# Seven products for the first up-projection pair of MLP groups 2 to 6, and second rounded copies in PSUM

## The chip, the cores and the metric

The kernel runs on one core of one Trainium2 chip. The metric is the device time of one execution in microseconds (us); less is better. Before the change it took 1220.0 us, the median of three runs (1218.8 to 1220.02). Five engines matter: TensorE (PE, with its weight loads as PEld) multiplies, VectorE (DVE) and ScalarE (ACT) do elementwise work, GpSimd (POOL) does elementwise work in parallel with them, and SyncE (SP) issues the transfers from HBM. Operands stand in SBUF; matmul results go to eight PSUM banks of 128 x 512 fp32 values.

## The reference

Two decoder layers on 512 tokens of width 1024: attention in layer 0, a gated short convolution in layer 1, each followed by the same MLP with 4096 hidden features, and a gated per-layer embedding. What the change touches is the MLP:

```
def sq_relu_mlp(h, w_up, w_down):
    return jnp.square(jax.nn.relu(h @ w_up)) @ w_down
for i in range(DEPTH):                              # DEPTH = 2
    ...                                             # mixer
    f = sq_relu_mlp(rmsnorm(x, g[2]), w_mlp_up[i], w_mlp_down[i])
    x = x + rmsnorm(f, g[3])
    ...                                             # gated embedding
```

Everything is fp32. The kernel reaches that precision on TensorE with rounded fp32 operands: each operand is split into a rounded part and the rest.

## The kernel before

**Three matmuls per product.** `mm3` (L268 to L270) multiplies hi by hi, lo by hi and hi by lo into one PSUM bank. So every weight tile and every activation has to be split: ACT makes the rounded copy (`wh`, L276), and DVE or POOL subtracts it from the source to give the rest (`wl`, L277). The subtraction reads two tiles in SBUF.

**The MLP in eight groups.** Each layer's MLP is worked in eight groups of 512 hidden features; group gr takes four feature blocks f = 0 to 3 of 128 features. Up-projection: for each f, eight depths k by three matmuls of 128 x 512 into one bank, 96 matmuls a group. Relu (L975) and square (L961) follow on ACT and leave `q`, 128 features by 512 tokens. Down-projection, groups 0 to 6: `q` is cut in token halves and feature halves, and the 2 x 2 block product is done by seven products instead of eight, in the order of `STEPS = (1, 2, 4, 5, 6, 7, 3)`. The names A11, A12, A22, S1 to S4 are blocks and sums of `q` (POOL makes the sums, L989, 128 x 256 each); B11 to B22 and T1 to T4 are blocks and differences of the down weights (POOL makes the differences, L168, 128 x 512). Each product takes two weight tiles p = 0, 1 and two banks s = 0, 1, 12 matmuls of 128 x 512, so 84 matmuls a group. DVE adds the result of each bank to an accumulator in SBUF (`acc`, L1021). After group 6 POOL combines the accumulators; group 7 is done with plain products.

**What sets the order.** Each weight tile has a place in one list. `prepare` loads and splits tiles up to `SOON` = 8 places ahead of the one that a matmul is about to use, and makes sums that the list needs when its first member comes up. SP loads the raw tiles into 14 buffers (`RAWS`). Split tiles, activations and sums live in 70 SBUF pages (`PAGES`). Instructions of one engine run in the order in which the scheduler puts them, and an instruction that waits holds up all that stand behind it on its engine. The sevens method also stands in layer 1's convolution, where `plan_sevens` (four weight blocks, four sums) serves 128 x 256 matmuls; the names `c_A`, `c_S`, `b_S` in the trace are of that place.

**Names in the trace.** `up` and `dn` are the PSUM banks of the two projections, `hTh` and `hTl` the split normalized input, `wh` and `wl` the split weights, `raw` a loaded tile, `dn_T` a difference of down weights, `r` the relu's and `q` the square's result, `s` a sum of blocks of `q`. In what follows D is the moment at which PE starts the down-projection of a group and U the moment at which it starts the next group's up-projection.

## Time and profile before

| | |
|---|---|
| device time, median of 3 runs | 1220.0 us |
| profiled execution, first to last instruction | 1216.5 us |
| PE busy | 1205.5 us (99%), 6175 matmuls |
| DVE busy | 931.4 us (77%), 1474 instructions |
| ACT busy | 691.4 us (57%), 1465 instructions |
| POOL busy | 655.4 us (54%), 616 instructions |
| transfers | 150.84 MB, 124 GB/s on average |

The profile shows one execution. Its own time is given as the span, 1216.5 us; the device time of the runs is 3.5 us longer at the median, which is what lies ahead of the first and behind the last instruction and the difference of one execution to another. Busy time is the time in which instructions of an engine ran. A row of a timeline names start, length, engine, line, operation, output and inputs, and in brackets how long the engine sat idle before it and what it waited for; a row with xN has N such instructions back to back. A group's row gives the sum of the busy time and the mean length in ns of one.

### The profile page before, as it was taken

Reading aid. Unit: us, or ns where it says so; the run is one execution under the profiler, and the core shown is the slowest. Engines: PE = TensorE matmul, PEld = TensorE weight load, DVE = VectorE, ACT = ScalarE, POOL = GpSimd, SP = SyncE. Lnnn points to the kernel's source line nnn. Section 1 sums busy time; section 2 is a strip of 40 time slices with the busy share of each in tenths; the row PEclk is TensorE's granted clock in tenths of the full one; section 3 lists DMA queues with packets and bytes.
Section 4 is the critical chain, followed back from the end, with each engine's and each line's share of the span. In section 5 each row is a group of like instructions: output and inputs, shape, how many; then the busy total and the mean of one; then the engine's idle time right before and its main releaser. Section 6 shows DMA issues by size and latency. Waiting matters only on the chain.

```text
span 1216.5 us, 18743 instructions
## 1 busy us (share of the span) xinstructions
PE 1205.5 (99%) x6175; PEld 1027.5 (84%) x6175; DVE 931.4 (77%) x1474; ACT 691.4 (57%) x1465; POOL 655.4 (54%) x616
## 2 busy tenths in 40 slices
PE   9999999999999999999999999999999999999997
PEld 8888887898888888888889999989888888888886
DVE  7888889586669766879877888866876787669873
ACT  7687778458644564455665534545746445645551
POOL 2035666155787877774213455126676878678210
PEclk9999999999999999999999999999999999999999
DMA  9376544623234323438223123542422443135401
GB/s 333 122 210 172 167 152 125 222 93 94 77 113 138 102 66 110 139 97 276 83 88 108 35 80 103 176 154 71 139 87 65 127 138 106 61 112 185 162 13 58
DMA packets 87314, 150.84 MB, mean 124 GB/s; under 512 B 10352, under 2 KB 18080, under 8 KB 87216
## 3 DMA queue, kind: packets, MB, share of 16 engines
q1 hardware_dynamic: 86640, 149.11, 39.3%
q8 instruction: 49, 0.80, 0.3%
q10 hardware_dynamic: 576, 0.53, 0.1%
q14 instruction: 49, 0.40, 0.1%
HBM read 139.03 MB, written 6.37 MB: 120 GB/s over the span
## 4 chain that ended last, share of the span: by engine, by line
PE 91%; ACT 3%; issue 2%; DVE 2%; POOL 1%; DMA 0%; SPq 0%; POOLq 0%; DVEq 0%; ACTq 0%
PE up L269 9%; PE up L270 9%; PE up L268 9%; PE dn L268 8%; PE dn L270 8%; PE dn L269 8%; PE v L476 3%; PE pg L269 2%; PE pg L268 2%; PE pg L270 2%; PE qk L270 2%; PE qk L269 2%; PE qk L268 2%; PE pT L590 1%; PE co L269 1%
## 5 line engine op out<-in xcount | busy, mean ns | idle before, releaser
L277 DVE TENSOR_TENSOR wl<-raw,wh 128x512 fp32r<-128x512 f32 x346 | 344.7, 1041 | 14.1 <-ACT wh L276 13.4
L269 PE MATMUL up<-hTh,wl 128*128 128x512 f32 (+1 forms) x576 | 210.2, 365 | 0.0
L270 PE MATMUL up<-hTl,wh 128*128 128x512 f32 (+1 forms) x576 | 209.6, 365 | 0.0
L268 PE MATMUL up<-hTh,wh 128*128 128x512 f32 (+1 forms) x576 | 208.7, 366 | 0.0
L276 ACT CAST wh<-raw 128x512 fp32r<-128x512 f32 x346 | 189.4, 625 | 4.5 <-DVE xd L373 4.4
L975 ACT ACTIVATE r<-up 128x512 f32<-128x512 f32 (+1 forms) x72 | 39.5, 548 | 201.8 <-PE up L270 190.1
L277 POOL TENSOR_TENSOR wl<-dn_T,wh 128x512 fp32r<-128x512 f32 x96 | 132.7, 1416 | 30.0 <-ACT wh L276 30.0
L168 POOL TENSOR_TENSOR dn_T<-raw,raw 128x512 f32<-128x512 f32 x56 | 87.0, 1564 | 69.1 <-DMA raw<-in_wdn 50.5
L269 PEld LDWEIGHTS up<-hTh,wl 128*128 128x128 f32 x576 | 108.6, 189 | 17.5
L268 PEld LDWEIGHTS up<-hTh,wh 128*128 128x128 f32 x576 | 108.6, 189 | 17.5
L270 PEld LDWEIGHTS up<-hTl,wh 128*128 128x128 f32 x576 | 108.2, 189 | 17.4
L1021 DVE TENSOR_TENSOR acc<-dn,acc 128x512 f32<-128x512 f32 x168 | 107.4, 680 | 13.9 <-PE dn L270 13.9
L168 POOL TENSOR_TENSOR dn_T<-raw,dn_T 128x512 f32<-128x512 f32 x56 | 92.5, 1651 | 2.2
L276 ACT CAST wh<-dn_T 128x512 fp32r<-128x512 f32 x112 | 61.4, 616 | 10.9 <-POOL dn_T L168 10.9
L277 DVE TENSOR_TENSOR A12l<-q,A12h 128x512 fp32r<-128x512 f32 x28 | 23.2, 829 | 53.8 <-ACT A12h L276 53.8
L1035 POOL TENSOR_TENSOR acc<-acc,acc 128x512 f32<-128x512 f32 x28 | 46.9, 1707 | 9.9 <-DVE acc L1021 9.9
L277 DVE TENSOR_TENSOR A11l<-q,A11h 128x256 fp32r<-128x256 f32 x28 | 23.2, 828 | 36.5 <-ACT A11h L276 36.5
L270 PE MATMUL qk<-hTl,wh 128*128 128x512 f32 x128 | 50.7, 396 | 0.0
L269 PE MATMUL pg<-wh,hTl 128*128 128x512 f32 x128 | 50.5, 394 | 0.0
L268 PE MATMUL pg<-wh,hTh 128*128 128x512 f32 x128 | 50.4, 394 | 0.0
L268 PE MATMUL qk<-hTh,wh 128*128 128x512 f32 x128 | 50.3, 393 | 0.0
L269 PE MATMUL qk<-hTh,wl 128*128 128x512 f32 x128 | 50.2, 392 | 0.0
(404 smaller groups left out, 3304.5 us busy)
## 6 DMA issues: line engine op xcount, KB each, us to landing
raw<-in_wup SPq DMA_DIRECT2D x128, 256.0 KB, 2.9
raw<-in_wdn SPq DMA_DIRECT2D x128, 256.0 KB, 2.8
raw<-in_wcq SPq DMA_DIRECT2D x36, 256.0 KB, 2.8
raw<-in_wqk SPq DMA_DIRECT2D x32, 256.0 KB, 5.3
raw<-in_wpg SPq DMA_DIRECT2D x32, 256.0 KB, 4.1
g<-in_g SPq DMA_DIRECT2D x22, 256.0 KB, 5.9
prl<-neg_c SPq DMA_DIRECT2D x16, 256.0 KB, 6.3
raw<-in_wo SPq DMA_DIRECT2D x16, 256.0 KB, 4.7
```

Of the source, the lines that this page charges most:

```text
L168: ins = nc.gpsimd.tensor_tensor(out=B[name], in0=B[a], in1=B[b], op=op)
L268: nc.tensor.matmul(ps, a.hi, b.hi, start=start, stop=False)
L269: nc.tensor.matmul(ps, a.lo, b.hi, start=False, stop=False)
L270: nc.tensor.matmul(ps, a.hi, b.lo, start=False, stop=stop)
L276: nc.scalar.copy(hi, src)
L277: return eng.tensor_tensor(out=lo, in0=src, in1=hi.bitcast(F32), op=ALU.subtract)
L476: nc.tensor.matmul(ps[:, : V_CHUNKS[c][1]], getattr(of_x(k, t), p), getattr(ready["v", c, k], of), start=k == 0 and p == of, stop=k == KT ...
L590: nc.tensor.transpose(ps[:, b * P : (b + 1) * P], probs[h][b][:, j * P : (j + 1) * P], ident)
L975: nc.scalar.activation(r[:, :n], ps[:, :n], AF.Relu)
L1021: ins = nc.vector.tensor_tensor(out=a, in0=banks[s], in1=a, op=ALU.add)
L1035: nc.gpsimd.tensor_tensor(out=a, in0=a, in1=acc[i, s][:, :S], op=ALU.add)
```

## The change

**Up-projection, groups 2 to 6 of both layers.** The first two feature blocks (f = 0, 1) are no longer done by 48 matmuls of 128 x 512, but by seven products of 128 x 256 each over four depths, 84 matmuls of 128 x 256 (`up_sevens`). Here the weights take the part of A: their four quarters come as A11, A12, A21, A22, and POOL makes four sums of them (S1 to S4). The tokens take the part of B: halves of the depth by halves of the tokens, with the differences T1 to T4, which POOL makes once a layer from copies that ACT takes when the input is normalized (`token_sums`, `quarters`). Three banks a, b, c receive the products; ACT copies one half bank to SBUF (`uu`) and DVE adds them up (`ud`, `uv`, `ud` again on half the columns, `um`), each reading one bank and one tile in SBUF. Relu and square follow on the two results `ud` and `um`, and `crossed` makes the sums for the down-projection from them. The second pair (f = 2, 3) is done as before.

**Second rounded copies.** For the weights of groups 2 to 6 that DVE splits, except those in `PLAINLY` (the sums S1 to S4 and the four raw tiles of the second pair), `split_beside` has ACT write the rounded copy twice, once to SBUF for the matmuls and once to one of two PSUM banks, from which the subtraction on DVE reads it. These two banks are held for a layer's MLP.

**Who does what.** T1 and T4 of the down weights are split by DVE there, T2 and T3 by POOL as before. POOL's differences come in another order (T1, T2, T4 of p = 0, then of p = 1, then both T3). DVE splits S1 to S4 of the up weights.

**Order on PE.** In groups 2 to 6 PE's instructions stand as the program writes them (`manual_schedule`). `PAGES` goes from 70 to 77, and the host lays out the weights of the first pair as quarters.

```diff
-PAGES = 70
+PAGES = 77
+BESIDE = range(2, 7)
+ON_VECTOR = ("T4", "T1")
+PLAINLY = {("up", "S1"), ("up", "S2"), ("up", "S3"), ("up", "S4"), *(("up", j) for j in range(4))}
+FIXED = range(2, 7)
+BACK = 6
+UP_SEVENS = range(2, 7)
+UP_FORMS = ("A11", "S2", "S1", "S3", "A12", "S4", "A22")
...
+                if key[0] == "up" or near(key) and key[3] in ON_VECTOR:
+                    eng = nc.vector
...
+            elif near(key) and eng is nc.vector and (key[0], key[-1]) not in PLAINLY:
+                split_beside(hi[:, :w], lo[:, :w], raw[:, :w], key[1])
...
+    def split_beside(hi, lo, src, l):
+        n = besides[l, "n"] = 1 - besides.get((l, "n"), 1)
+        if (l, n) not in besides:
+            besides[l, n] = bank(f"beside{l}_{n}")
+        copy = besides[l, n][:, : src.shape[-1]]
+        nc.scalar.copy(copy.bitcast(F32R), src)
+        nc.scalar.copy(hi, src)
+        nc.vector.tensor_tensor(out=lo, in0=src, in1=copy, op=ALU.subtract)
...
+        def up_sevens(gr):
+            L, R = slice(0, S // 2), slice(S // 2, S)
+            a, b, c = (bank(f"up{l}_{gr}_{s}") for s in "abc")
+            u, v, d, m = (page(f"u{s}{l}_{gr}") for s in "uvdm")
...
+            def product(ps, form, tokens):
+                for k in range(4):
+                    w = wide("up", l, 2 * gr, form, soon=SOON + MORE).at(lambda h: h[:, k * P : (k + 1) * P])
+                    mm3(ps, w, second(tokens, k), k == 0, k == 3)
+
+            product(c[:, L], "A11", "B11")
+            nc.scalar.copy(u[:, L], c[:, L])
+            product(a[:, R], "S2", "T2")
+            product(b[:, L], "S1", "T1")
+            product(b[:, R], "S3", "T3")
+            product(a[:, L], "A12", "B21")
...
+            add(two(d[:, :S]), two(a), both(u[:, L]))
+            add(two(v[:, :S]), two(b), both(d[:, R]))
+            add(d[:, R], b[:, L], v[:, R])
+            product(c[:, L], "S4", "B22")
+            product(c[:, R], "A22", "T4")
+            add(m[:, :S], c, v[:, :S])
...
-            up(gr, done)
-            down(gr, A)
+            with ExitStack() as order:
+                if gr in FIXED:
+                    order.enter_context(tc.manual_schedule(engines={mybir.EngineType.PE}))
+                up(gr, done)
+                down(gr, A)
```

**DVE where one group ends and the next begins.** In layer 0, before the change, from the last additions of group 3's down-projection to the first split of group 4's activations (`acc0_7_1` is product 7, bank 1):

```order
L1021 TENSOR_TENSOR acc0_7_1_4278<-dn0_3_71_5479,acc0_7_1_4278 128x512
L1021 TENSOR_TENSOR acc0_3_0_4306<-dn0_3_30_5506,acc0_3_0_4306 128x512
L1021 TENSOR_TENSOR acc0_3_1_4308<-dn0_3_31_5507,acc0_3_1_4308 128x512
L277 TENSOR_TENSOR wl164_5572<-raw140_5539,wh164_5571 128x512
L277 TENSOR_TENSOR wl165_5582<-raw141_5541,wh165_5581 128x512
L277 TENSOR_TENSOR wl166_5592<-raw142_5543,wh166_5591 128x512
L277 TENSOR_TENSOR wl167_5602<-raw143_5545,wh167_5601 128x512
L277 TENSOR_TENSOR A11l0_4_0_5615<-q0_4_0_5534,A11h0_4_0_5614 128x256
```

The same place on DVE after the change, between groups 4 and 5 (the entries to groups 2 to 6 have it so, in layer 1 with `acc0_3_0` one row earlier):

```order
L1138 TENSOR_TENSOR acc0_7_1_4338<-dn0_4_71_6215,acc0_7_1_4338 128x512
L296 TENSOR_TENSOR wl188_6179<-up_0_10_S2_6161,wh188_6178 128x512
L296 TENSOR_TENSOR wl189_6193<-up_0_10_S1_6159,wh189_6192 128x512
L1138 TENSOR_TENSOR acc0_3_0_4372<-dn0_4_30_6239,acc0_3_0_4372 128x512
L296 TENSOR_TENSOR wl190_6203<-up_0_10_S3_6163,wh190_6202 128x512
L312 TENSOR_TENSOR wl191_6217<-raw149_6153,beside0_0_4698 128x512
L1138 TENSOR_TENSOR acc0_3_1_4374<-dn0_4_31_6240,acc0_3_1_4374 128x512
L296 TENSOR_TENSOR wl192_6228<-up_0_10_S4_6165,wh192_6227 128x512
L312 TENSOR_TENSOR wl193_6242<-raw151_6157,beside0_1_4748 128x512
L296 TENSOR_TENSOR wl194_6253<-raw152_6254,wh194_6252 128x512
L296 TENSOR_TENSOR wl195_6281<-raw153_6282,wh195_6280 128x512
L296 TENSOR_TENSOR wl196_6300<-raw154_6301,wh196_6299 128x512
```

On DVE it goes on without a row left out, up to the addition `um`:

```order
L296 TENSOR_TENSOR wl197_6318<-raw155_6319,wh197_6317 128x512
L312 TENSOR_TENSOR wl198_6368<-raw156_6335,beside0_0_4698 128x512
L312 TENSOR_TENSOR wl199_6385<-raw157_6337,beside0_1_4748 128x512
L1053 TENSOR_TENSOR ud0_5_6278<-up0_5_a_6273,uu0_5_6276 128x512
L1053 TENSOR_TENSOR uv0_5_6277<-up0_5_b_6274,ud0_5_6278 128x512
L312 TENSOR_TENSOR wl200_6405<-raw158_6339,beside0_0_4698 128x512
L312 TENSOR_TENSOR wl201_6422<-raw159_6341,beside0_1_4748 128x512
L1053 TENSOR_TENSOR ud0_5_6278<-up0_5_b_6274,uv0_5_6277 128x256
L1053 TENSOR_TENSOR um0_5_6279<-up0_5_c_6275,uv0_5_6277 128x512
```

Where seven instructions stood ahead of the first split of an activation, twenty-one now stand: the splits of the second pair's raw tiles and of four of the next down weights are ahead of the addition `um`, and eight of the twenty-one read two tiles in SBUF (L296), the others one tile in SBUF and one PSUM bank.

**ACT in the up-projection of group 4.** Before the change:

```order
L975 ACTIVATE r0_4_0_0_5611<-up0_4_0_0_5538 128x512
L961 ACTIVATE q0_4_0_5534<-r0_4_0_0_5611 128x512
L276 CAST A11h0_4_0_5614<-q0_4_0_5534 128x256
L975 ACTIVATE r0_4_1_0_5645<-up0_4_1_0_5620 128x512
L961 ACTIVATE q0_4_1_5535<-r0_4_1_0_5645 128x512
L276 CAST A12h0_4_1_5648<-q0_4_1_5535 128x512
L276 CAST S1h0_4_1_5656<-s120_4_1_5652 128x512
L276 CAST S3h0_4_1_5660<-s340_4_0_5618 128x512
```

After the change:

```order
L1077 ACTIVATE rd0_4_5949<-ud0_4_5788 128x512
L1077 ACTIVATE rm0_4_5951<-um0_4_5789 128x512
L996 ACTIVATE q0_4_0_5777<-rd0_4_5949 128x512
L996 ACTIVATE q0_4_1_5778<-rm0_4_5951 128x512
L295 CAST A11h0_4_0_5955<-q0_4_0_5777 128x512
L295 CAST A12h0_4_0_5959<-q0_4_1_5778 128x256
L295 CAST S1h0_4_0_5969<-s120_4_0_5963 128x512
L295 CAST S3h0_4_0_5973<-s340_4_0_5964 128x512
L1016 ACTIVATE r0_4_2_0_6002<-up0_4_2_0_5977 128x512
L996 ACTIVATE q0_4_2_5779<-r0_4_2_0_6002 128x512
L295 CAST A11h0_4_2_6005<-q0_4_2_5779 128x256
L1016 ACTIVATE r0_4_3_0_6036<-up0_4_3_0_6011 128x512
```

The relus of the first pair no longer read a bank that PE has just finished, but sums that DVE makes, and the relus of the second pair (L1016) stand behind all that comes from `um`.

**DVE at the start of group 4's down-projection (D).** Before the change DVE's rows from the split of A12 on, without the two T4 tiles, which POOL splits:

```order
L277 TENSOR_TENSOR A12l0_4_3_5743<-q0_4_3_5537,A12h0_4_3_5742 128x512
L277 TENSOR_TENSOR S1l0_4_3_5751<-s120_4_3_5746,S1h0_4_3_5750 128x512
L1021 TENSOR_TENSOR acc0_1_0_4134<-dn0_4_10_5758,acc0_1_0_4134 128x512
L1021 TENSOR_TENSOR acc0_1_1_4136<-dn0_4_11_5759,acc0_1_1_4136 128x512
L277 TENSOR_TENSOR S3l0_4_3_5755<-s340_4_2_5712,S3h0_4_3_5754 128x512
L1021 TENSOR_TENSOR acc0_2_0_4160<-dn0_4_20_5782,acc0_2_0_4160 128x512
```

After the change:

```order
L296 TENSOR_TENSOR A12l0_4_3_6040<-q0_4_3_5780,A12h0_4_3_6039 128x512
L1138 TENSOR_TENSOR acc0_1_1_4166<-dn0_4_11_6076,acc0_1_1_4166 128x512
L296 TENSOR_TENSOR S1l0_4_3_6048<-s120_4_3_6043,S1h0_4_3_6047 128x512
L296 TENSOR_TENSOR S3l0_4_3_6052<-s340_4_2_6009,S3h0_4_3_6051 128x512
L312 TENSOR_TENSOR wl177_6056<-dn_0_4_T4_0_5865,beside0_1_4748 128x512
L312 TENSOR_TENSOR wl178_6061<-dn_0_4_T4_1_5871,beside0_0_4698 128x512
L1138 TENSOR_TENSOR acc0_2_0_4196<-dn0_4_20_6099,acc0_2_0_4196 128x512
```

The two T4 tiles (`wl177`, `wl178`), which the third product of the down-projection needs, now stand on DVE behind the last split of an activation, `S3l`.

More of the change, by code (lines that the diff above doesn't have):

```diff
@@ L234, in trunk @@
             for i in range(2):
+                tiles = [wup[l, 2 * gr + i, j] for j in range(4)]
+                if i == 0 and gr in UP_SEVENS:
+                    plan_sevens(("up", l, 2 * gr), tiles, UP_FORMS)
+                    continue
                 for j in range(4):
-                    plan(("up", l, 2 * gr + i, j), wup[l, 2 * gr + i, j])
+                    plan(("up", l, 2 * gr + i, j), tiles[j])
             if gr < 7:
@@ L955, in conv, with mlp @@
         return lambda k, t: tokens_of(ys[k], t)
-    def mlp(l, hT, xs, then, late):
+    def mlp(l, hT, xs, then, late, full):
         acc, lows = {}, {}
@@ L966, in up @@
                 for f in range(4):
+                    if f < 2 and gr in UP_SEVENS:
+                        if f == 0:
+                            done(f, 0, S, *up_sevens(gr))
+                        continue
                     need(*range(lo // P, hi // P), *(range(NB) if f == 3 else ()))
@@ L976, in up, with token_sums @@
                     done(f, lo, hi, r)
+                    if gr == 1:
+                        next(aside, None)
+                    if gr in FIXED:
+                        prepare(where["up", l, 2 * gr + 1, 3] + 1 + (SOON if f == 3 else SOON - BACK + 2))
+        T = {}
+        def token_sums():
+            for name, a, b in (("T1", "B12", "B11"), ("T2", "B22", "T1"),
+                               ("T3", "B22", "B12"), ("T4", "B21", "T2")):
+                for q in range(2):
+                    full[name, q] = page(f"{name}f{l}_{q}")
+                    t = full[name, q][:, :S]
+                    nc.gpsimd.tensor_tensor(
+                        out=t, in0=full[a, q][:, :S], in1=full[b, q][:, :S], op=ALU.subtract
+                    )
+                    T[name, q] = Pair(*(page(f"{name}{s}{l}_{q}", F32R) for s in "hl"))
+                    split(T[name, q].hi[:, :S], T[name, q].lo[:, :S], t)
+                    yield
@@ L1200, in trunk, with quarters @@
     xs = [load_x("xb", t) for t in range(NB)]
+    full = {}
+    def quarters(t, n, ps):
+        for q in range(2):
+            at = f"B{n + 1}{t // 2 + 1}", q
+            if t % 2 == 0:
+                full[at] = page(f"{at[0]}f{q}")
+            to = full[at][:, :S].rearrange("p (k c) -> p k c", k=2)
+            nc.scalar.copy(
+                to[:, :, t % 2 * P : (t % 2 + 1) * P],
+                ps[:, q * 256 : q * 256 + 256].rearrange("p (k c) -> p k c", k=2),
+            )
     for l in range(2):
@@ L1296, in layout @@
     up, dn = np.asarray(w_mlp_up), np.asarray(w_mlp_down)
-    got["wup"] = np.stack([tiles(up[l], 2, 256) for l in range(2)])
+    plain = np.stack([tiles(up[l], 2, 256) for l in range(2)])
+    sevens = up.reshape(2, 2, 4, P, FF // 256, 2, P).transpose(0, 4, 5, 1, 3, 2, 6)
+    is7 = np.array([i % 2 == 0 and i // 2 in UP_SEVENS for i in range(FF // 256)])
+    got["wup"] = np.where(is7[:, None, None, None], sevens.reshape(plain.shape), plain)
     got["wdn"] = np.stack([tiles(dn[l], 1, S) for l in range(2)])
```

70 lines of the change are left out of this document (50 added, 20 removed).

## The prediction, made before the changed kernel was run

> **What bounds the kernel now.** I read the busy times first, then the chain that ended last:
>
> ```profile
> PE 1205.5 (99%) x6175; PEld 1027.5 (84%) x6175; DVE 931.4 (77%) x1474; ACT 691.4 (57%) x1465; POOL 655.4 (54%) x616
> PE 91%; ACT 3%; issue 2%; DVE 2%; POOL 1%; DMA 0%; SPq 0%; POOLq 0%; DVEq 0%; ACTq 0%
> ```
>
> PE works in 99% of the span, and 91% of the chain is PE's own. An average can hide a stage, so next come windows of one MLP group each (columns: window, its length, busy us of PE, PEld, DVE, ACT, POOL, granted clock, DMA share, GB/s):
>
> ```profile
> core 0: us, PE busy (x) PEld busy (x) DVE busy (x) ACT busy (x) POOL busy (x), PEclk, DMA share, GB/s
> 443.00:483.80 40.80, 40.80 (x182) 33.80 (x181) 28.94 (x36) 20.83 (x39) 30.99 (x24) 1.00 0.34 103
> 483.80:524.60 40.80, 40.80 (x182) 33.80 (x181) 29.17 (x36) 20.84 (x39) 30.75 (x24) 1.00 0.34 104
> ```
>
> PE is busy for the whole group at full clock: 96 + 84 = 180 matmuls in 40.80 us, 0.2267 us each. The others have 10 to 20 us to spare, so only fewer PE cycles can shorten a group, and work elsewhere matters only once PE waits for it.
>
> **The change part by part: PE.** The cadence of both sizes, from the timeline (start, length; starts twelve matmuls apart):
>
> ```profile
> 436.79 0.39 PE L268 MATMUL up<-hTh,wh 128*128 128x512 f32 x1
> ...
> 439.28 0.39 PE L270 MATMUL up<-hTl,wh 128*128 128x512 f32 x1
> 439.51 0.39 PE L268 MATMUL dn<-wh,A11h 128*128 128x512 f32 x1
> ...
> 700.03 0.28 PE L268 MATMUL c_A<-T4h,wh 128*128 128x256 f32 x1
> ...
> 701.35 0.28 PE L270 MATMUL c_A<-T4l,wh 128*128 128x256 f32 x1
> ```
>
> 512 columns: 2.49/11 = 0.226 us. 256 columns, in layer 1's sevens: 1.32/11 = 0.120 us. Removed 48 x 0.2267 = 10.88 us, added 84 x 0.120 = 10.08 us: **-0.80 us a group**, -8.0 us for the ten groups. A group is then 40.0 us: up 20.96 (10.08 + 10.88), down 19.04 (seven steps of 2.72). That is small against what follows.
>
> The Trainium skill ("TensorE: Matmul & The Clock Gate", section "Back-to-back issue gap") lists 262 cycles for 256 columns and 518 for 512, at 2.4 GHz 109 and 216 ns. By it the saving would be 1.2 us a group (an estimate); the rows are from this kernel's own stream, so I keep 0.80.
>
> **The start of the down-projection.** D, its first matmul, is 439.51. The chain from f3's last matmul to the last activation split:
>
> ```profile
> 439.71 0.60 ACT L975 ACTIVATE r<-up 128x512 f32<-128x512 f32 x1 [2.48 <-PE up L270]
> 440.34 0.63 ACT L961 ACTIVATE q<-r 128x512 f32<-128x512 f32 x1
> 441.00 0.62 ACT L276 CAST A12h<-q 128x512 fp32r<-128x512 f32 x1
> 441.05 0.74 POOL L989 TENSOR_TENSOR s<-q,q 128x256 f32<-128x256 f32 x1 [0.97 <-ACT q L961]
> 441.87 1.08 POOL L989 TENSOR_TENSOR s<-s,q 128x256 f32<-128x256 f32 x1
> 443.02 0.74 POOL L989 TENSOR_TENSOR s<-q,s 128x256 f32<-128x256 f32 x1
> 443.80 0.62 ACT L276 CAST S3h<-s 128x512 fp32r<-128x512 f32 x1 [0.20 <-POOL s L989]
> 443.63 0.69 DVE L277 TENSOR_TENSOR S1l<-s,S1h 128x512 fp32r<-128x512 f32 x1 [1.28 <-ACT S1h L276]
> 444.33 2.18 ACT L276 CAST wh<-dn_T 128x512 fp32r<-128x512 f32 x4
> 445.02 6.04 POOL L277 TENSOR_TENSOR wl<-dn_T,wh 128x512 fp32r<-128x512 f32 x4 [1.25 <-ACT wh L276]
> ```
>
> S3h ends at D+4.9. With the new order DVE then splits S3 (to D+5.6) and the first T4 tile, which ends near D+6.25. PE wants its rest in the third matmul of step 3, at 2 x 2.72 + 2 x 0.2267 = D+5.89. That is a wait of about **0.4 us a group**. Bounds: 0, should S3's split come forward, and 1.4, should that split meet POOL and take twice its time. Before, the scheduler ran other matmuls there; now PE's order is fixed. Other operands of the down-projection have 0.3 us (T1) to over 1 us to spare.
>
> **DVE's train ahead of `um`.** The relus, squares, sums and splits of f0 and f1 all hang on the addition `um`, behind twenty DVE instructions that follow product 7's second addition. Eight read two tiles in SBUF ("S": four up sums, four raw tiles), twelve read one tile and one bank ("P", one of half length). What each takes, from the tile and timeline views (in the first two rows columns: count, min/median/max ns, first to last start):
>
> ```profile
> L277 DVE TENSOR_TENSOR wl<-raw,wh x346: 673/685/1844, 157.0 to 1175.0; 128x512 fp32r<-128x512 f32 x173
> L1021 DVE TENSOR_TENSOR acc<-dn,acc x168: 674/678/692, 323.3 to 1118.0; 128x512 f32<-128x512 f32 x168
> 565.71 4.29 DVE L277 TENSOR_TENSOR wl<-raw,wh 128x512 fp32r<-128x512 f32 x7
> 457.44 4.07 DVE L277 TENSOR_TENSOR wl<-raw,wh 128x512 fp32r<-128x512 f32 x3
> 457.44 3.52 POOL L168 TENSOR_TENSOR dn_T<-raw,dn_T 128x512 f32<-128x512 f32 x2
> 461.43 2.47 DVE L1021 TENSOR_TENSOR acc<-dn,acc 128x512 f32<-128x512 f32 x4
> 460.93 3.00 POOL L168 TENSOR_TENSOR dn_T<-raw,raw 128x512 f32<-128x512 f32 x2
> 463.83 5.21 DVE L277 TENSOR_TENSOR wl<-raw,wh 128x512 fp32r<-128x512 f32 x4
> 463.89 3.46 POOL L168 TENSOR_TENSOR dn_T<-raw,dn_T 128x512 f32<-128x512 f32 x2
> 505.95 4.12 DVE L277 TENSOR_TENSOR wl<-raw,wh 128x512 fp32r<-128x512 f32 x4
> 504.75 3.03 POOL L168 TENSOR_TENSOR dn_T<-raw,dn_T 128x512 f32<-128x512 f32 x2
> 452.65 1.31 POOL L168 TENSOR_TENSOR dn_T<-raw,raw 128x512 f32<-128x512 f32 x1 [1.59 <-issue]
> ```
>
> With POOL still, an S takes 4.29/7 = 0.61 us. Beside POOL's differences it takes 4.07/3 = 1.36, 5.21/4 = 1.30, and 1.03 where POOL covers three quarters of the stretch. A P beside POOL keeps 2.47/4 = 0.62. So the time of an S, here s, decides. POOL has four up sums and eight differences to make back to back from about U-5.5 (the place of the 452.65 row, U = D+19.04), 12 x 1.3 to 1.74 = 16 to 21 us: it is busy through the whole train. I take **s = 1.30**; the bounds are 0.61 and 1.84.
>
> The Trainium skill ("SBUF — State Buffer", section "Who interferes with whom") says that a DVE instruction with two SBUF inputs contends with a GpSimd instruction that reads SBUF, for an exclusive lock, and that one with a single SBUF input does not; the two kinds of rows agree.
>
> Product 7's second bank is done at U-2.95, its addition 0.43 later and 0.61 long: the train starts at U-1.9. `um` ends at U - 1.9 + 8s + 11 x 0.61 + 0.35 = U + 5.16 + 8s. With 1.30 that is **U+15.6**; its bank c would be ready for an end at U+10.9.
>
> **What is late next.** Behind `um` ACT does the relu and two squares (about 1.8), POOL four sums (3.5: the three rows' 2.71 and one more), ACT the copy of S3 (0.66), and only then the second pair's relu, square and A11 copy (0.60, 0.66, 0.44): 7.6 us, because ACT's order puts them behind S3. f3's relu could start at D+0.20 = U+21.16. So `um` may come at U+13.5; at U+15.6 f3's relu is **2.0 us late**, and with it, link by link, S3 and the T4 split.
>
> Sum for a group: 40.8 - 0.8 + 0.4 + 2.0 = 42.4, which is +1.6; ten groups +16. On the profiled 1216.5 that is 1232.5; the median run lies 3.5 us above this span: **1236 us**.
>
> **Edits put at nothing.** ACT gains thirteen second copies of 0.55 (2.18/4), three more rounded copies and a half copy, about 9 us a group, to 30 of 40: its free 20 us hide them, except where the order puts them ahead of a relu. POOL loses four splits (6.04 us) and gains four sums (about 6). The token differences are 8 x 1.5 = 12 us of POOL a layer during groups 0 and 1, where POOL has 10 us free in each; were that cover gone, some 2 us a layer. The copies with the norms (16 of about 0.3 us) fall into ACT's idle time there; uncovered they cost 5 us a layer. Pages change no duration.
>
> **The rivals.**
>
> *Light contention* (0.29). If POOL waits for its tiles, s falls. The page has such waits:
>
> ```profile
> L168 POOL TENSOR_TENSOR dn_T<-raw,raw 128x512 f32<-128x512 f32 x56 | 87.0, 1564 | 69.1 <-DMA raw<-in_wdn 50.5 <-DVE acc L1021 6.1 <-DVE wl L277 3.6
> ```
>
> 50.5 us over 14 groups are 3.6 a group, and the last down tiles reuse buffers that the train frees. With s up to 1.04 nothing is late: 40.4 a group, 1216 us; without the T4 wait too, 1212. Against it: in the new order four up sums, whose tiles come first, fill the start.
>
> *No change* (0.06). 40.8 again if `um` is 0.4 late, at U+13.9: s = 1.10. A narrow spot between the two.
>
> *Strict turns* (0.07). If each S waits for a whole POOL instruction when it follows another S (four of eight: 1.31 + 0.61 = 1.92) and half of one otherwise (1.26), s is 1.59, `um` comes at U+17.9, 4.4 late: +4.0 a group, 1260 us. The longest S in the row, 1844, speaks for it; the runs at 1.30 and 1.36 speak against.
>
> *The sevens do not shorten PE* (within the last chance). Were a 256-column matmul held to the length of its weight load, 0.19 us (33.80/181), the pair would take 15.7 us, +4.9 a group and over 1265. The 0.120 in layer 1 excludes it.
>
> **How the numbers follow.** The forecast, contention that delays the second pair, has 0.58. Its own range, s from 1.15 to 1.45, is +0.4 and +2.8 a group: 1224 to 1248. Light contention adds the stretch down to 1212. The strict turns stay outside, so the range is 1211 to 1249. Two runs of this kernel can be told apart from about 0.2%, 2.4 us: faster 0.29, same 0.06, slower 0.65 (0.58 + 0.07).
>
> **What would show it.** In the changed profile a group should have PE gaps of about 2.4 us, most of them at step 3 of the down-projection and none in the up-projection; S splits near U of 1.2 to 1.4 us mean next to 0.68 for those from a bank; `um` ending 15 to 16 us after U; ACT idle before the second pair's S3 copy on POOL's sums. The prediction is wrong if `um` ends before U+13.5, or if PE waits elsewhere: on a PSUM bank, which six banks for matmuls would show, or on ACT's second copies.

## The result, and the profile after

The changed kernel takes **1277.12 us** (median of four runs, 1275.85 to 1277.64) against 1220.01 for the one before beside it: 57 us slower, a ratio of 1.0473 with a 95% interval of 1.0458 to 1.0488. The side was as predicted; the size was not (+16 forecast, and the range ended at 1249).

The page of the changed kernel, busy times and chain, in the form of the rows shown of before:

```profile
PE 1224.5 (96%) x6535; PEld 1044.4 (82%) x6535; DVE 992.7 (78%) x1600; ACT 796.4 (62%) x1683; POOL 683.5 (54%) x632
```

```profile
PE 54%; DVE 15%; ACT 10%; POOL 10%; issue 8%; DMA 2%; SPq 0%; POOLq 0%; DVEq 0%; ACTq 0%
```

PE was 91% of the chain and is 54%: the end is now set by work that PE waits for, on DVE, ACT and POOL. Where the time went, by windows that begin with the first matmul of a stage (columns as in the prediction; first groups 2 to 6 of layer 0 and of layer 1, then groups 0 and 1 of both). Before:

```profile
336.15:540.15 204.00, 204.00 (x902) 168.97 (x900) 149.36 (x183) 104.16 (x190) 156.91 (x122) 1.00 0.35 107
904.08:1108.08 204.00, 204.00 (x901) 168.97 (x900) 152.05 (x183) 104.16 (x190) 156.18 (x121) 1.00 0.35 106
250.56:336.15 85.59, 85.46 (x474) 74.05 (x472) 62.24 (x71) 56.35 (x115) 55.16 (x49) 1.00 0.28 88
819.02:904.08 85.06, 85.06 (x473) 74.19 (x472) 61.82 (x70) 55.86 (x114) 55.42 (x49) 1.00 0.28 86
```

After:

```profile
349.01:567.99 218.98, 207.27 (x1082) 174.26 (x1081) 182.78 (x236) 150.20 (x281) 152.69 (x121) 0.99 0.32 99
945.21:1166.40 221.19, 210.73 (x1081) 179.31 (x1080) 180.04 (x239) 151.48 (x281) 151.38 (x121) 0.96 0.32 98
252.12:349.01 96.89, 89.22 (x473) 74.88 (x472) 63.61 (x80) 62.30 (x135) 75.30 (x58) 0.98 0.23 74
849.76:945.21 95.45, 89.28 (x474) 74.88 (x473) 63.20 (x77) 60.39 (x129) 74.75 (x58) 0.98 0.23 72
```

| stage | before | after | difference | predicted |
|---|---|---|---|---|
| groups 2 to 6, both layers | 408.0 | 440.2 | +32.2 | +16 |
| groups 0 and 1, both layers | 170.6 | 192.3 | +21.7 | 0 |
| the rest of the span | 637.9 | 642.4 | +4.5 | 0 |
| span | 1216.5 | 1274.9 | +58.4 | +16 |

**Groups 2 to 6.** One of them, up-projection and down-projection apart:

```profile
437.36:458.34 20.98, 20.98 (x134) 19.09 (x132) 18.14 (x21) 11.41 (x22) 14.86 (x11) 1.00 0.51 165
458.34:481.40 23.06, 21.11 (x86) 16.79 (x84) 17.69 (x27) 18.66 (x35) 15.61 (x15) 0.93 0.14 42
```

The up-projection takes 20.98, as worked out (20.96), without a gap. The down-projection takes 23.06 where 19.04 is its matmuls' time, and PE's granted clock there is 0.93. DVE's timeline of the same group, U = 437.36:

```profile
435.45 3.39 DVE L296 TENSOR_TENSOR wl<-up_S,wh 128x512 fp32r<-128x512 f32 x2
438.76 0.68 DVE L1138 TENSOR_TENSOR acc<-dn,acc 128x512 f32<-128x512 f32 x1
...
442.90 6.29 DVE L296 TENSOR_TENSOR wl<-raw,wh 128x512 fp32r<-128x512 f32 x4
449.11 1.27 DVE L312 TENSOR_TENSOR wl<-raw,beside 128x512 fp32r<-128x512 f32 x2
...
453.15 0.68 DVE L1053 TENSOR_TENSOR um<-up_c,uv 128x512 f32<-128x512 f32 x1
```

The two kinds are as told apart: splits from two SBUF tiles take up to 1.70 us each, from a bank 0.60 from start to start. Over the ten groups the eight splits average 1.26 to 1.41 (1.30 taken), and `um` ends 15.9 to 16.5 us after U (17.8 and 17.9 in the first group of each layer; 15.6 predicted). What follows on ACT and PE, D = 458.34:

```profile
459.92 0.59 ACT L1016 ACTIVATE r<-up 128x512 f32<-128x512 f32 x1
460.54 0.63 ACT L996 ACTIVATE q<-r 128x512 f32<-128x512 f32 x1
461.20 0.40 ACT L295 CAST A11h<-q 128x256 fp32r<-128x256 f32 x1
461.51 0.59 ACT L1016 ACTIVATE r<-up 128x512 f32<-128x512 f32 x1
```

```profile
459.47 0.39 PE L289 MATMUL dn<-wl,A11h 128*128 128x512 f32 x1
461.66 0.50 PE L287 MATMUL dn<-wh,A11h 128*128 128x512 f32 x1 [1.80 <-ACT A11h L295]
...
462.90 0.63 PE L289 MATMUL dn<-wl,A11h 128*128 128x512 f32 x1
463.33 0.63 PE L287 MATMUL dn<-wh,A11h 128*128 128x512 f32 x1
```

f3's relu starts at D+3.2, 3.0 late (2.0 predicted). PE stops 1.80 us for A11 of f2, and then the matmuls start 0.43 us apart instead of 0.227 for some seven of them. These slow matmuls, with no wait beside their rows, I had not foreseen. Six of the ten groups have such a stretch and lose 1.6 to 1.8 us each by the spacing of the starts, some 10 us in all; the four others keep the full clock and lose 0.3 to 0.4 in single late starts.

**Groups 0 and 1.** In group 0's down-projection POOL makes the token differences (first three rows), and DVE's splits beside them take 1.73 us each (next two):

```profile
289.77 3.42 POOL L1032 TENSOR_TENSOR T2f<-B22f,T1f 128x512 f32<-128x512 f32 x2
293.15 3.43 POOL L1032 TENSOR_TENSOR T3f<-B22f,B12f 128x512 f32<-128x512 f32 x2
296.54 1.73 POOL L1032 TENSOR_TENSOR T4f<-B21f,T2f 128x512 f32<-128x512 f32 x1
290.28 3.46 DVE L296 TENSOR_TENSOR wl<-dn_T,wh 128x512 fp32r<-128x512 f32 x2
295.36 3.46 DVE L296 TENSOR_TENSOR wl<-dn_T,wh 128x512 fp32r<-128x512 f32 x2
292.10 0.50 PE L289 MATMUL dn<-wl,S1h 128*128 128x512 f32 x1 [1.03 <-DVE wl L296]
297.19 0.50 PE L289 MATMUL dn<-wl,S3h 128*128 128x512 f32 x1 [1.04 <-DVE wl L296]
```

PE waits four times for such a split. In group 1 the last difference stands on POOL behind that group's weight differences, and its split on ACT stands ahead of the second feature block's relu:

```profile
321.55 1.29 POOL L1032 TENSOR_TENSOR T4f<-B21f,T2f 128x512 f32<-128x512 f32 x1
322.87 0.62 ACT L295 CAST T4h<-T4f 128x512 fp32r<-128x512 f32 x1 [8.81 <-POOL T4f L1032]
323.40 0.59 ACT L1016 ACTIVATE r<-up 128x512 f32<-128x512 f32 x1
332.21 1.12 PE L287 MATMUL dn<-wh,A11h 128*128 128x512 f32 x2 [1.44 <-ACT A11h L295]
```

ACT stands still for 8.81 us, the last of the four relus starts at 332.06, 7 us after the down-projection (325.08), and PE waits there for the operands that follow. The token copies cost something too: in layer 0 four rows of them, 274.22 to 276.24, stand on ACT ahead of group 0's last relus, and the second half of its up-projection takes 16.8 us instead of 14.5 (15.6 in layer 1), also in second_spread70 below, where no difference stands in group 0 (16.8 and 15.7). That is 3.5 of the 21.7 us.

### The profile page after: what moved, and what is told of

It reads as the page before. It is cut to its first block, busy times and chain, and to the rows that moved or that the text cites. A ratio compares the mean times of both kernels' runs of the same rounds, so it can differ in the third digit from the quotient of the medians.

```text
span 1274.9 us, 19756 instructions
## 1 busy us (share of the span) xinstructions
PE 1224.5 (96%) x6535; PEld 1044.4 (82%) x6535; DVE 992.7 (78%) x1600; ACT 796.4 (62%) x1683; POOL 683.5 (54%) x632
## 4 chain that ended last, share of the span: by engine, by line
PE 54%; DVE 15%; ACT 10%; POOL 10%; issue 8%; DMA 2%; SPq 0%; POOLq 0%; DVEq 0%; ACTq 0%
DVE wl L296 7%; PE dn L288 5%; PE dn L289 5%; PE dn L287 5%; POOL s L1108 3%; POOL dn_T L179 2%; POOL s L1091 2%; PE v L511 2%; DVE wl L312 2%; PE qk L288 2%; PE qk L287 2%; PE qk L289 2%; DVE acc L1138 2%; PE up L287 2%; PE up L289 2%
## 5 line engine op out<-in xcount | busy, mean ns | idle before, releaser
L296 DVE TENSOR_TENSOR wl<-raw,wh 128x512 fp32r<-128x512 f32 x246 | 237.9, 1010 | 12.4 <-ACT wh L295 12.0
L287 PE MATMUL up<-hTh,wh 128*128 128x512 f32 (+1 forms) x416 | 148.1, 358 | 2.5 <-ACT r L1016 2.5
L288 PE MATMUL up<-hTh,wl 128*128 128x512 f32 (+1 forms) x416 | 147.8, 357 | 0.0
L289 PE MATMUL up<-hTl,wh 128*128 128x512 f32 (+1 forms) x416 | 147.4, 357 | 0.0
L310 ACT CAST beside<-raw 128x512 fp32r<-128x512 f32 x90 | 53.0, 589 | 81.1 <-DVE wl L312 78.9
L296 POOL TENSOR_TENSOR wl<-dn_T,wh 128x512 fp32r<-128x512 f32 x56 | 71.2, 1302 | 40.0 <-ACT wh L295 40.0
L287 PEld LDWEIGHTS up<-hTh,wh 128*128 128x128 f32 x416 | 78.6, 189 | 14.3 <-ACT r L1016 3.3
L288 PEld LDWEIGHTS up<-hTh,wl 128*128 128x128 f32 x416 | 78.6, 189 | 11.0
L296 DVE TENSOR_TENSOR A11l<-q,A11h 128x256 fp32r<-128x256 f32 (+1 forms) x28 | 21.1, 752 | 49.2 <-ACT A11h L295 49.2
L312 DVE TENSOR_TENSOR wl<-raw,beside 128x512 fp32r<-128x512 f32 x90 | 58.4, 676 | 0.0
L287 PE MATMUL dn<-wh,A11h 128*128 128x512 f32 x76 | 32.5, 437 | 23.0 <-ACT A11h L295 21.8
L1152 POOL TENSOR_TENSOR acc<-acc,acc 128x512 f32<-128x512 f32 x28 | 45.8, 1667 | 10.3 <-DVE acc L1138 10.3
```

What stands on the lines that cost most here:

```text
L287: nc.tensor.matmul(ps, a.hi, b.hi, start=start, stop=False)
L288: nc.tensor.matmul(ps, a.lo, b.hi, start=False, stop=False)
L289: nc.tensor.matmul(ps, a.hi, b.lo, start=False, stop=stop)
L296: return eng.tensor_tensor(out=lo, in0=src, in1=hi.bitcast(F32), op=ALU.subtract)
L310: nc.scalar.copy(copy.bitcast(F32R), src)
L312: nc.vector.tensor_tensor(out=lo, in0=src, in1=copy, op=ALU.subtract)
```

## The experiments

Theory: three losses that hardly touch each other, (1) contention ahead of `um` with a slow clock behind the gap it makes, (2) token differences, (3) something small in the rest. Rival: the second copies on ACT and their two banks, where the waits of the changed kernel show

```profile
ACT beside L310 <- DVE wl L312: 82.0, 45, 5.2
```

(82.0 us in all, 45 times, 5.2 the longest). The edits are against the changed kernel unless said otherwise; each ratio is to the kernel before on the same chip.

**Second copies for the second pair too (second_beside).**

```diff
-PLAINLY = {("up", "S1"), ("up", "S2"), ("up", "S3"), ("up", "S4"), *(("up", j) for j in range(4))}
+PLAINLY = {("up", "S1"), ("up", "S2"), ("up", "S3"), ("up", "S4")}
```

> The four raw tiles of the second pair get a second rounded copy in PSUM too, so that four of the eight DVE splits ahead of um no longer read two tiles in SBUF. Theory (contention of DVE and POOL delays um): um ends about 4 x (1.7 - 0.6) = 4.4 us earlier, near U+12, f3's relu is not late, a group takes 40.4 to 40.8 instead of 43.0 to 45.1; about 33 us less than the change, near 1244. Rival (ACT held up by the two banks: in the trace of the change it waits 82 us for DVE's splits there): four more copies through the same banks, 1277 or more.

Measured: 1254.7 us, ratio 1.0287 (1.0272 to 1.0303), 22 us less than the change. `um` ends near U+14.1, f3's relu is 0.9 late, seven groups take 41.4 to 41.6 and three 42.7; the time is 11 us above the expected one.

```profile
479.44 2.62 DVE L312 TENSOR_TENSOR wl<-raw,beside 128x512 fp32r<-128x512 f32 x4
483.20 2.03 DVE L312 TENSOR_TENSOR wl<-raw,beside 128x512 fp32r<-128x512 f32 x3 [1.14 <-ACT beside L310]
```

Seven splits take 5.8 us with the wait, where the four plain ones alone had taken 6.3. Contention is a cause, and the rival's sign is refuted; but the second row shows why U+12 was missed: DVE waits 1.14 us for ACT's copy into a bank, so the two banks do cost, in a smaller way.

**No second copies (no_beside).**

```diff
-            elif near(key) and eng is nc.vector and (key[0], key[-1]) not in PLAINLY:
+            elif False:
```

> The change with no second copies at all and no banks held for them; every split on DVE reads two tiles in SBUF, fourteen of the twenty ahead of um instead of eight. Theory (contention): um at U - 1.9 + 14 x 1.36 + 5 x 0.61 + 0.35 = U+20.5, 4 us later than in the change, a group 4 us longer, near 1317. Rival (the second copies on ACT and their two banks are the cause): 1260 or less.

Measured: 1317.2 us, ratio 1.0796 (1.0777 to 1.0814). The time is as expected, the way to it only in part: fourteen splits averaged 1.04 to 1.23 each, not 1.36, and `um` ended mostly between U+18 and U+19.2, not at U+20.5; the rest of the 45 to 53 us a group was lost elsewhere. In its trace PE waits 13.9 us for plain splits on DVE in the down-projections, in 14 waits of up to 3.6 us, where the changed kernel has 7.1 in eight; what else adds up is open. What stands is that the second copies help here; without them the kernel is 40 us slower still.

**A gap filled with matmuls (filled).**

```diff
+FILL = 9
...
+                if i == 1 and gr in FIXED:
+                    idle = bank(f"idle{l}_{gr}")
                 for p in range(2):
                     w = wide("dn", l, gr, b_name, p)
+                    if i == 1 and p == 1 and gr in FIXED:
+                        for _ in range(FILL):
+                            nc.tensor.matmul(idle, A["A11", 0].at(lambda h: h[:, :P]).hi, ready["dn", l, gr, "B11", 0].hi, start=True, stop=True)
```

> The change with nine additional matmuls of 128 x 512 (9 x 0.227 = 2.0 us) into a spare bank between the two weight tiles of the first product of the down-projection in groups 2 to 6, where PE waits 1.2 to 2.0 us and then runs several matmuls at 0.43 us each. Theory (a gap of that length lowers the granted clock): the matmuls fill the gap, the slow ones disappear (10 us in ten groups by the trace), the wait itself stays; near 1267. Rival (the slow matmuls wait for operands): their 2.0 us fill the gap but change nothing behind it, 1277 to 1280.

Measured: 1283.3 us, ratio 1.0523 (1.0507 to 1.0538), 6 us slower than the change, outside both expectations. Two of its down-projections:

```profile
459.06:481.51 22.45, 21.98 (x94) 17.20 (x93) 17.68 (x27) 17.40 (x32) 15.00 (x15) 1.00 0.10 30
1147.09:1173.10 26.01, 23.64 (x95) 18.29 (x93) 20.68 (x30) 19.48 (x36) 16.11 (x14) 0.93 0.23 71
```

Where the gap is filled, the clock is 1.00 and the down-projection takes 22.45 instead of 23.06, although 2.0 us of additional matmuls stand in it: the slow matmuls are the granted clock after a pause, not operands. Seven groups are like the first row. The whole is no faster, since in the others (group 2 of both layers and the last one, second row) a wait of 1.6 to 2.1 us for T4's split came up later in the group, in two of the three with slow matmuls behind it: these three lose 7 us against the changed kernel, and the seven gain 1.5.

**The token work alone (sums_alone)**, on the kernel before:

```diff
-PAGES = 70
+PAGES = 77
...
+                    if gr == 1:
+                        next(aside, None)
...
+        aside = token_sums()
...
             for i in STEPS:
+                next(aside, None)
...
-            kind, lhs, xs, g1, lambda t: pre_norm(t, xs[t], g2, hT, f"n2{l}"), opened
+            kind, lhs, xs, g1, lambda t: pre_norm(t, xs[t], g2, hT, f"n2{l}", quarters), opened
```

> The kernel before with nothing but the token copies (ACT, with the norms) and the token differences and their splits (POOL, ACT, DVE in groups 0 and 1); nothing uses them. Theory (what groups 0 and 1 lost, 21.7 us, and some 4 us around the norms come from these): 26 us slower than before, near 1246. Rival (groups 0 and 1 lose by the weights prepared for group 2, the two held banks or the fixed order): at most 8 us slower, below 1228.

Measured: 1247.4 us, ratio 1.0227 (1.0210 to 1.0244): 28 us with nothing gained, of which 24 lie in the first four groups of the two layers. **And everything but the token work (no_sums)**:

```diff
-                return T[name, k // 2].at(lambda u: u[:, k % 2 * 256 : k % 2 * 256 + 256])
+                return hT.at(lambda u: u[:, k, 0:256])
...
-        aside = token_sums()
...
-            kind, lhs, xs, g1, lambda t: pre_norm(t, xs[t], g2, hT, f"n2{l}", quarters), opened
+            kind, lhs, xs, g1, lambda t: pre_norm(t, xs[t], g2, hT, f"n2{l}"), opened
```

> The change without token copies and token differences: the products read halves of the split input where T1 to T4 belong, so this part of the computation is left out. Theory (the token differences cost 26 to 28 us by themselves, the rest is groups 2 to 6): 1249 to 1251, all ten groups as in the change. Rival (the two parts overlap or feed each other): outside 1244 to 1256.

Measured: 1252.5 us, ratio 1.0268 (1.0249 to 1.0287), and groups 0 and 1 are back: the second half of group 0's up-projection takes 14.47 and its down-projection 19.07. The two runs lose 28.0 and 32.8 us, 60.8 together; both contain the 3.5 us of the pages (below), and 60.8 - 3.5 = 57.3 is what the change loses. The parts add up.

**The token differences on another engine and later (sums_late).**

```diff
-                    nc.gpsimd.tensor_tensor(
+                    nc.vector.tensor_tensor(
                         out=t, in0=full[a, q][:, :S], in1=full[b, q][:, :S], op=ALU.subtract
...
             for i in STEPS:
-                next(aside, None)
+                if gr == 1:
+                    next(aside, None)
```

> The change with the eight token differences of a layer on DVE instead of POOL, and all of them in group 1 (one per feature block, one per step of the down-projection), none in group 0. Theory (in group 0 POOL's differences run against DVE's splits, and in group 1 the last one, behind POOL's weight differences, holds ACT): the downs of groups 0 and 1 lose 4.0, 6.1, 4.9 and 3.1 us less, about 1259. Rival (the work itself is too much there, wherever it stands): 1272 or more.

Measured: 1288.9 us, ratio 1.0565 (1.0549 to 1.0581), slower than the change. Group 0's down-projection is back at 19.07, but group 1's takes 31.8, and group 2's up-projection 26.6 instead of 21.0. ACT, in order, waits for the differences:

```profile
335.12 0.62 ACT L295 CAST T3h<-T3f 128x512 fp32r<-128x512 f32 x1 [4.77 <-DVE T3f L1032]
```

The time is the one that the rival named, not the theory's 1259. Group 0 shows that its loss came from the differences that stood there; but the edit changes the engine and the place at once, so it cannot tell whether the work is too much or stands badly. What tells that is the run spread below, where the same work, on POOL at another place, costs about half.

**Pages (pages_only)**, the kernel before with the two sizes alone, the pages and the scratch for DMA descriptors, which the change made smaller too:

```diff
-PAGES = 70
+PAGES = 77
-    nc = bacc.Bacc("TRN2", target_bir_lowering=False, num_devices=1)
+    nc = bacc.Bacc("TRN2", target_bir_lowering=False, num_devices=1, dynamic_dma_scratch_size=1024)
```

> The kernel before with nothing but 77 pages in place of 70 and the smaller descriptor scratch. Some 4 us were lost in the first convolution products and 1 us at the start, in every kernel with 77 pages, also in the one without token copies. Theory (the larger pool lets the scheduler order other stages otherwise, and that costs): 1223 to 1225. Rival (pages change nothing, the 4 us come from the MLP's end): 1220.

Measured: 1223.5 us, ratio 1.0029 (1.0019 to 1.0039): 3.5 us by the ratio. The two profiled executions are 5.6 us apart, and 4.5 of these lie between the two layers' MLPs, in windows from group 7 of layer 0 to group 0 of layer 1. Before, and with 77 pages:

```profile
540.15:819.02 278.87, 278.59 (x1641) 247.47 (x1640) 225.19 (x328) 141.77 (x306) 97.72 (x90) 1.00 0.40 125
```

```profile
541.31:824.64 283.33, 280.89 (x1641) 248.93 (x1640) 223.01 (x328) 141.57 (x306) 95.96 (x90) 0.99 0.39 123
```

The same matmuls, 2.4 us of PE gaps instead of 0.3, and a lower clock. That the scheduler orders instructions otherwise with more pages is the likely reason and was only argued, and which of the two sizes does it was not told apart.

**`um` ahead of the next down weights (um_ahead).**

```diff
-MORE = 0
+MORE = -4
```

> The look-ahead of the seven products is 4 places instead of 8 (MORE = -4), which puts the splits of four of the next down weights behind um on DVE; contention stays. Theory (what counts is when um ends): um 4 x 0.6 = 2.4 us earlier, near U+14, the wait at the start of the down-projection shrinks from 2 to 3 us to below 1, the clock stays full after it; about 41.1 a group, near 1249. Rival (the wait at D is for something else, or the four splits are now late themselves): within 5 us of 1277.

Measured: 1316.5 us, ratio 1.0798 (1.0782 to 1.0814): a clear miss. `um` did come, at U+10.97, as early as its bank allows, and the splits took 0.68 us, since POOL was still. But the look-ahead also calls for POOL's eight weight differences. They now start behind the sums that follow `um`, with U = 444.04 and D = 465.02:

```profile
459.63 0.74 POOL L1108 TENSOR_TENSOR s<-q,s 128x256 f32<-128x256 f32 x1
460.33 1.76 POOL L179 TENSOR_TENSOR dn_T<-raw,raw 128x512 f32<-128x512 f32 x1
...
469.20 2.50 POOL L179 TENSOR_TENSOR dn_T<-raw,raw 128x512 f32<-128x512 f32 x2
```

and end 6.7 us after D: a group takes 48. The test still tells that a still POOL removes the contention. **The same with the differences called for earlier, on second_beside (early_sums).**

```diff
             product(c[:, R], "A22", "T4")
+            derive(("dn", l, gr))
```

> second_beside with the look-ahead of the seven products at 4 places, but the differences of the next down weights called for right after the last product, not with their first split. Theory (in um_ahead the gain was lost because POOL's eight differences started some 10 us later and stood ahead of the sums behind um): differences done by about U+14, um near U+12, a group 40.4 to 40.8 instead of 41.4 to 42.8 in second_beside, near 1245. Rival (the differences wait for their tiles, whose buffers the delayed splits free): 1270 or more.

Measured: 1276.0 us, ratio 1.0459 (1.0444 to 1.0475), worse than second_beside by 21, and neither reason given: the differences end by U+13, `um` at U+10.97, f3's relu is 0.2 us late in most groups, and PE now waits 0.5 and 1.6 to 3.4 us for T4's split, which DVE does behind S1, S3 and two additions; in seven of the ten groups slow matmuls follow.

**T4's split.** Four runs on that: emitted one feature block earlier, on second_beside (t4_ahead) and on early_sums (early_t4), and the same with T4 split by POOL as before the change (t4_pool_second, t4_pool; only they have the second edit).

```diff
+AT_TWO = 4
...
-                        prepare(where["up", l, 2 * gr + 1, 3] + 1 + (SOON if f == 3 else SOON - BACK + 2))
+                        prepare(where["up", l, 2 * gr + 1, 3] + 1 + (SOON if f == 3 else SOON - BACK + AT_TWO))
...
-ON_VECTOR = ("T4", "T1")
+ON_VECTOR = ("T1",)
```

> second_beside with T4's splits emitted after the third feature block instead of the fourth, so that on DVE they stand ahead of the last S1 and S3 splits. Theory (what second_beside still waits for in the down-projection is T4's split, 0.4 to 0.5 us and a slow clock behind it): a group 40.8 in place of 41.4, about 6 us less than second_beside, near 1249. Rival (f3's relu, 0.9 us late there, sets the end): within 2 us of 1254.7.

> early_sums with the same edit for T4. There um ended at U+10.97, as early as its bank allows, f3's relu was 0.2 to 0.9 us late, and PE still waited 0.5 and 1.7 to 3.4 us for T4's split. Theory (that is the last wait, and the slow clock follows it): a group 40.2 to 40.5 in place of 44.0, near 1240. Rival (the wait moves to T1 or S1): a group over 42, 1255 or more.

Measured: 1255.1 us (1.0289, 1.0274 to 1.0304) and 1290.3 us (1.0577, 1.0561 to 1.0593). The wait for T4 is gone in both, but f3's relu starts at D+2.1 and D+2.5 in most groups: ACT now has T4's copies ahead of it. Both times are the rivals', not the theories' (1249 and 1240); and second_beside has no stretch of half clock in groups 2 to 6, so behind its T4 wait none was to be won back.

> early_t4 with T4's splits on POOL, from an SBUF copy, as in the kernel before. In early_t4 and t4_ahead PE no longer waited for T4, but the second copies of T4 on ACT stood ahead of f3's relu and waited for a bank, so the relu came at D+2.5 and D+2.1. Theory (what is left per group is ACT's order around the two banks): f3's relu near D+0.4, a group 40.2 to 40.6 in place of 45, near 1242. Rival (T1's second copies or POOL's longer list take the place): a group over 42, 1258 or more.

> t4_ahead with T4's splits on POOL. Theory (ACT's order around the two banks): f3's relu near D+1.0 in place of D+2.1, groups 40.5 to 41.0 in place of 42, near 1244. Rival (um, at U+12.8 to U+14.6 there, decides): within 4 us of 1255.

Measured: 1252.1 us (1.0264, 1.0249 to 1.0279) and 1244.0 us (1.0201, 1.0184 to 1.0218). The second is as expected, the first 10 us above. In t4_pool most groups take 41.1. The wait for T4 is gone, but f3's relu is still at D+2.5 (D = 451.25), now behind T1's second copies:

```profile
452.18 1.11 ACT L311 CAST beside<-dn_T 128x512 fp32r<-128x512 f32 x2
453.23 0.62 ACT L296 CAST wh<-dn_T 128x512 fp32r<-128x512 f32 x1
453.75 0.60 ACT L1017 ACTIVATE r<-up 128x512 f32<-128x512 f32 x1
```

In t4_pool_second eight of ten groups take 40.2 to 40.6. One of those without any gap of PE:

```profile
430.58:451.56 20.98, 20.98 (x133) 19.09 (x132) 15.63 (x24) 16.43 (x33) 14.85 (x13) 1.00 0.56 164
451.56:470.77 19.21, 19.21 (x85) 15.69 (x84) 14.78 (x24) 13.96 (x27) 16.46 (x15) 1.00 0.15 45
```

40.19 against 40.80 before: the seven products do save 0.6 us a group once nothing waits.

**The token differences in the up-projections of groups 1 and 2 (spread, on early_t4; t4_pool_spread70, on t4_pool with 70 pages; second_spread70, on t4_pool_second with 70 pages).** BESIDE and FIXED go from range(2, 7) to range(3, 7) too, and each difference's split is emitted one call later than the difference.

```diff
-UP_SEVENS = range(2, 7)
+UP_SEVENS = range(3, 7)
...
-                    if gr == 1:
-                        next(aside, None)
+                    if gr in (1, 2):
+                        for _ in range((1, 2, 2, 0)[f]):
+                            next(aside, None)
```

> early_t4 with sevens, second copies and fixed order in groups 3 to 6 only, and the token differences on POOL in the up-projections of groups 1 and 2, each split one step behind its difference. Theory (there POOL, ACT and DVE have slack, and none of the differences holds ACT): groups 0 to 2 lose 4 us a layer at most instead of 11, eight groups at 40.3, 1220 + 5 + 8 - 4 = near 1229. Rival (the differences cost wherever they stand, as in the run that moved them to DVE): 1240 or more.

> t4_pool with sevens in groups 3 to 6 only, the token differences on POOL in the up-projections of groups 1 and 2, and 70 pages as before. Theory: the run spread lost 5 us a layer in groups 0 to 2, pages_only 3.5 us in all; eight groups at 40.4 give -3: 1220 + 10 - 3 = near 1227. Rival (groups over 42 as in spread): 1240 or more.

> t4_pool_second, whose later groups took 40.2 to 40.6, with sevens in groups 3 to 6 only, the token differences on POOL in the up-projections of groups 1 and 2, and 70 pages. Theory (the parts add): 1220 + 10 for token copies and differences + 2 x 1.6 for the first group of each layer - 6 x 0.4 = near 1231, still above the kernel before. Rival (token differences at this place disturb the first of these groups as in t4_pool_spread70, where it took 43.6): 1235 or more.

Measured: 1270.1 (1.0413, 1.0398 to 1.0429), 1240.5 (1.0171, 1.0155 to 1.0186) and 1234.5 us (1.0126, 1.0109 to 1.0143), where 1229, 1227 and 1231 were expected. In spread the groups with sevens take 44 to 46.5, as in early_t4. At this place the token work costs groups 0 to 2 some 5 to 7 us a layer instead of 11 in groups 0 and 1, and with 70 pages the stretch between the MLPs is back at 278.85. In the last run the later groups take 40.1 to 40.9, but the first with sevens takes 44.2 and 43.4, with `um` only at U+17.2 and U+16.4. It is the fastest version found with the sevens, and 15 us slower than the kernel before: by windows groups 0 to 2 lose 10.3, the two first groups 6.0, and the six others gain 1.8. No run came below the kernel before.

## Why the prediction was right in its side and wrong in its size

- **PE's saving, -0.80 a group: right.** The up-projections take 20.98 (20.96 worked out), and t4_pool_second and second_spread70 show whole groups at 40.1 to 40.2 (40.0 worked out).
- **Contention as the mechanism: right, and nearly in size.** s 1.26 to 1.41 for 1.30, `um` U+15.9 to U+16.5 for U+15.6, A11 of f2 7.8 us behind it for 7.6, f3's relu 2.4 to 3.0 us late for 2.0, in eight groups. In the first group of each layer it was 3.9 and 4.4. *Light contention* is refuted: s stayed above the 1.04 that it needs, and POOL waited for its tiles 0.45 us in the group shown. *Strict turns* is near to what a row of plain splits does (1.6 to 1.7 each, where 1.92 was worked out), but the eight together did not. One reading was off without effect: the row at 452.65 of before is U-5.9, not U-5.5.
- **The wait at T4, 0.4 at step 3: misplaced.** PE waits first at A11 of f2, in step 1, and in the four groups that keep the full clock 0.3 to 0.4 us of the T4 wait follow. Of gaps, 2.4 us a group were expected and 1.9 to 4.1 came, by the spacing of the starts.
- **What a gap does to the clock: missing from the sum**, some 10 us. With the somewhat later `um` this makes the 3.2 us a group, where 1.6 were forecast.
- **"Edits put at nothing", the token differences: the step that failed.** I compared 12 us of POOL with 20 us of its idle time and priced lost cover at 2 us a layer, a figure with no sum behind it. Together with the token copies they cost 28 us with the pages, some 24 without. Idle time in sum was no cover: in group 0 they run against plain splits of DVE, at 1.73 us each, and in group 1 one of them holds ACT for 8.81 us. The copies, put at nothing for ACT's idle time, cost 3.5 us in group 0, where they stand ahead of relus.
- **"Pages change no duration": wrong by 3.5 us.**

By windows, 16 of the missing 42 us lie in groups 2 to 6, 21.7 in groups 0 and 1 and 4.5 in the rest. The side was no luck: groups 2 to 6 alone lost 32 us, and the contention ahead of `um` that was forecast stands behind them; its 16 us were half of that.

## What to carry to other kernels

Work put at nothing because an engine has idle time must be placed, not summed: name the instruction it stands ahead of on every in-order engine it passes through (POOL, ACT and DVE here), and whether the engine beside it is then reading two SBUF tiles. On a kernel whose PE never paused, price each new pause with the slow matmuls that can follow it (1.6 to 1.8 us here). And when one queue entry is moved, look at what else the same call brings along: each mended wait here (`um`, T4, the relu) uncovered the next one on ACT or POOL.

## What the runs showed of the hardware that was not expected

After a pause of PE of 1.8 us the matmuls of 512 columns can start 0.43 us apart instead of 0.227, with a granted clock of 0.93 over that down-projection (the window from 458.34 above); with the pause filled it was 1.00. But the same pause, 1.80 us by its row, did nothing to the clock one group earlier:

```profile
418.11 0.50 PE L287 MATMUL dn<-wh,A11h 128*128 128x512 f32 x1 [1.80 <-ACT A11h L295]
```

The record of the granted clock tells the two apart. In the changed kernel every stretch of half clock in groups 2 to 6 lasts 3.41 us, and any two of them start a whole number of 3.413 us apart (462.06, 970.65, 1015.02, 1059.39, 1103.77 and 1148.14; each of the last four steps is 13 times that). In windows cut on this grid, the two of the earlier group and the two of the later one:

```profile
414.27:417.68 3.41, 2.04 (x10) 1.35 (x8) 1.52 (x3) 2.39 (x5) 1.46 (x2) 1.00 0.01 2
417.68:421.10 3.42, 2.84 (x11) 2.16 (x12) 2.19 (x3) 2.35 (x5) 2.38 (x4) 1.00 0.00 0
458.65:462.06 3.41, 1.61 (x7) 0.86 (x5) 1.81 (x3) 3.15 (x6) 1.44 (x2) 1.00 0.00 0
462.06:465.47 3.41, 3.26 (x9) 2.52 (x9) 2.10 (x5) 1.91 (x4) 2.47 (x3) 0.50 0.00 0
```

The earlier pause is cut in two by the grid, with 1.37 us of idle PE in one window and 0.58 in the next; the later one lies whole in one window, with 1.80, and the next window has half the clock. In the ten groups the windows ahead of the six slow ones hold 1.50 to 2.87 us of idle PE, and no other window more than 1.46. So where a pause falls decides as much as its length. The line is not sharp: in no_sums a window with 1.74 us idle (488.59 to 492.01) was not followed by a slow one. No run moved a pause to test this.

The Trainium skill ("TensorE: Matmul & The Clock Gate", section "What's actually happening") has the clock halve after an idle window of some 3.4 us, with windows that run freely. The halving agrees (0.43 against 0.227), and so do the windows (3.41 us, on one grid through the whole trace); but no window had to be idle as a whole: 1.50 us of one were enough.

In the up-projection of group 1 one POOL difference took 8.49 us, while DVE ran twelve splits from two SBUF tiles back to back without being slowed (the last six are shown):

```profile
302.92 8.49 POOL L179 TENSOR_TENSOR dn_T<-raw,raw 128x512 f32<-128x512 f32 x1 [4.65 <-DMA raw<-in_wdn]
...
306.57 3.69 DVE L296 TENSOR_TENSOR wl<-raw,wh 128x512 fp32r<-128x512 f32 x6
```

POOL's instruction ended at 311.41, 1.15 us behind DVE's last split, and alone it takes some 1.3. So the two engines seem not always to take turns: here 0.61 us a split for DVE and nothing for POOL, elsewhere up to 1.70 for each. What decides which it is was not tried, nor that nothing else held POOL there.
